# FFN down products of four pairs of blocks by seven half-size products, and squares of the first norm on ScalarE, in a two-layer fp32 decoder trunk

## The chip, the cores and the metric

One core of a Trainium2 chip runs the whole trunk. The metric is the device time of one execution in microseconds; the kernel before has a median of 1934.61 us over 3 runs (1933.79 to 1934.62).

## What is computed

```python
for l in range(DEPTH):                      # DEPTH = 2
    x = x + 0.5 * swiglu(rmsnorm(x, ffn1_norm[l]), ffn1_w_gate[l], ffn1_w_up[l], ffn1_w_down[l])
    x = x + hybrid_mixer(rmsnorm(x, mix_norm[l]), ...)
    x = x + 0.5 * swiglu(rmsnorm(x, ffn2_norm[l]), ffn2_w_gate[l], ffn2_w_up[l], ffn2_w_down[l])

def swiglu(x, w_gate, w_up, w_down):
    return (jax.nn.silu(x @ w_gate) * (x @ w_up)) @ w_down
```

512 tokens, model width 1024, FFN width 2816, everything in float32. There are four FFNs (two a layer). The mixer (sparse attention beside an mLSTM) is not touched.

## The kernel before

Activations are kept transposed: channels on the 128 partitions, the 512 tokens along the free axis, so x is 8 tiles of 128x512 and a matmul streams tokens past a 128x128 piece of weights. To keep float32 accuracy every operand is split in two parts, `hi` (a rounded copy, made by ScalarE) and `lo` (the rest, by a subtraction on VectorE), and every product is three matmuls: hi·hi, hi·lo, lo·hi.

**Weights** come as units of 128x1024 numbers. `fetch` (line 229) loads a unit on SP's queue into a ring of six raw buffers; `unit` (line 263) makes up to two units ahead of the one that it hands out: ScalarE writes `whi` (line 272), VectorE writes `wlo` (line 277). whi and wlo have three buffers each, so the conversion of a unit waits until TensorE is done with the unit three places before it.

**The FFN** is cut into 11 blocks of 256 hidden channels. Blocks 0 and 1 use plain products (`up_plain`). Blocks 2 to 10 compute gate and up in one go by Winograd's form of Strassen's scheme (`quad`, line 476; its list is PRODUCTS): seven products of 24 matmuls of 256 columns, in place of eight. The sums of weight quarters that the scheme needs (s1 to s4) are made by GpSimd on raw units (`form`, line 249: four 128x1024 operations a block); the sums of token parts (t1 to t4) are made once an FFN by `combine`. `assemble` reads the PSUM banks on ScalarE and VectorE, applies Silu and the product of gate and up (`put`, line 498), and splits h into hi and lo (lines 499, 500).

**Groups.** GROUPS pairs the blocks: (0), (1, 2), (3, 4), (5, 6), (7, 8), (9, 10). The down product of a pair is four plain units (`ffn_down`, line 532): each makes two output tiles of 128x512 from four pieces of h, 24 matmuls of 512 columns, and VectorE adds each tile to x straight from PSUM (line 545). `ffn_plan` (line 188) places the four units of a pair between the seven products of the two blocks of the next pair.

**Order.** TensorE runs in the order in which the code is written. On the other engines a scheduling layer sorts by priority (`high_priority` raises it); each engine then works strictly in the order that comes out. `norm` (line 315) squares x, sums the squares on GpSimd (line 334) and splits x times the gain; in the first norm of the program the squares are made by VectorE (line 330), elsewhere by ScalarE (line 332).

In the text a **period** is the stretch from the first product of the first block of one of the pairs (3, 4), (5, 6), (7, 8), (9, 10) to the same place of the next one. Each period holds 14 products and the down work of the pair before. There are four in an FFN and 16 in all.

Of the kernel before, what the change touches and what calls it, by code (L numbers as in the profile page):

```python
# [42 lines left out]
DOWNS = {(1, 1): (), (5, 0): ((3, 0), (5, 1)), (5, 1): ((7, 2), (7, 3))}  # L43
# [16 lines left out]
class Trunk:  # L60
# [5 lines left out]
    def run(self):  # L66
        tc = self.tc
        with tc.tile_pool(name="const", bufs=1) as self.cp, \
# [8 lines left out]
            with tc.manual_schedule(engines={mybir.EngineType.PE}):  # L77
                for l in range(DEPTH):
                    self.norm(self.g1[l], LAG["ffn"] if l else LAG["ffn0"], l == 0)
# [30 lines left out]
    def setup(self):  # L110
        nc, cp, t = self.nc, self.cp, self.t
        self.x = []
# [46 lines left out]
        with self.tc.high_priority(offset=20000):  # L159
            for i in range(NKT):  # L160
                xt = cp.tile([P, S], F32, name=f"x{i}", tag=f"x{i}")
                nc.sync.dma_start(xt, t["x"][i])
                self.x.append(xt)
                if i in START:
                    self.fetch()
# [22 lines left out]
    def ffn_plan(self):  # L188
        plan = [("U", 0, i) for i in range(4)]
        plan += [("U", 1, 0), ("U", 1, 1), ("D", 0, 0), ("D", 0, 1), ("U", 1, 2), ("U", 1, 3)]  # L190
        for gi in range(1, len(GROUPS)):
            for i, b in enumerate(GROUPS[gi]):
                if b == 1:
                    continue
                at = DOWNS.get((gi, i), ((3, 0), (5, 1)) if i == 0 else ((2, 2), (5, 3)))
                for p in range(7):
                    plan += [("D", gi - 1, u) for n, u in at if n == p]
                    plan.append(("Q", b, p))
                plan += [("D", gi - 1, u) for n, u in at if n == 7]
# [10 lines left out]
    def ffn_units(self, l, n):  # L210
        t = self.t
        for kind, b, i in self.plan:
# [3 lines left out]
            elif kind == "D":  # L216
                self.add(t["wda" + n][l, i] if b == 0 else t["wdb" + n][l, b - 1, i], dma=b == 0)
            else:
# [21 lines left out]
    def plain(self, i, n):  # L240
        return self.got(i)[:, :n]

# [72 lines left out]
    def norm(self, g, ffn=0, first=False):  # L315
# [6 lines left out]
        for i in range(NKT):  # L322
# [95 lines left out]
    def ffn(self):  # L418
        h = {}
        quad = None  # L420
        for kind, b, i in self.plan:
            gi = b if kind == "D" else (b + 1) // 2
            if kind != "D" and gi not in h:
                nf = 2 * len(GROUPS[gi])
                tags = ("zah", "zal") if gi % 2 else ("kT", "big")
                h[gi] = None
            if kind == "U":
# [3 lines left out]
                if i == 3:  # L431
                    if b == 0:
                        h[gi] = [self.ap_.tile([P, 2, S], F32R, name="h0", tag="s4b", bufs=2) for _ in range(2)]
                        with self.tc.high_priority(offset=500):
                            self.gate_plain(ps, h[gi])
                    else:
                        h[gi] = [self.ap_.tile([P, nf, S], F32R, name=t, tag=t) for t in tags]
                        next(self.rest)
# [709 lines left out]
```

## Time and profile before

| | |
|---|---|
| median of 3 runs | 1934.61 us |
| the profiled execution | 1933.71 us |
| its span, first to last instruction | 1931.9 us |
| TensorE busy | 98% of the span |
| VectorE, ScalarE, GpSimd busy | 71%, 50%, 28% |
| granted TensorE clock, mean | 0.994 of full speed |

The profiled execution is within 0.05% of the median. The 1.8 us between its own time and its span lie outside the first and last instruction. Matmuls overlap one another, so the duration of one (283 ns for 256 columns) is longer than its distance to the next; what counts is the distance.

### The profile page before, as it was taken

How to read it: one execution, taken by the hardware profiler on the slowest of the kernel's cores; microseconds unless marked ns; L12 is line 12 of the kernel's file. 1: busy time of each engine (PE TensorE's matmuls, PEld its weight loads, DVE VectorE, ACT ScalarE, POOL GpSimd, SP SyncE). 2: the span in 40 equal slices, each digit the busy share in tenths (PEclk: the TensorE clock that was granted, in tenths of full speed). 3: DMA queues.
4: the chain of work that ended last, by engine and by line, in shares of the span. 5: the costliest groups of instructions: out<-in, count | busy, mean ns of one | idle time of the engine just before them, and what ended most of it. 6: DMA issues, size and time to landing. Idle time of an engine off the chain costs nothing.

```text
span 1931.9 us, 29548 instructions
## 1 busy us (share of the span) xinstructions
PE 1898.5 (98%) x11712; PEld 1703.2 (88%) x11712; DVE 1381.1 (71%) x2228; ACT 957.8 (50%) x1495; POOL 543.8 (28%) x335
## 2 busy tenths in 40 slices
PE   7999999999999999999999999999999999999999
PEld 5899999887888899999989999998877888999997
DVE  5976666679955876666788666665898558766665
ACT  3543434477775544343454343435777655434332
POOL 3433323212112242324124423322211122432330
PEclk8999999999999999999999999999999999999999
DMA  6423323375446622323353323334744465332322
GB/s 200 119 83 115 109 88 118 109 159 126 88 91 154 158 99 77 130 78 120 110 141 89 120 79 118 104 110 127 157 107 87 104 142 130 109 118 80 130 68 88
DMA packets 63067, 219.28 MB, mean 114 GB/s; under 512 B 8272, under 2 KB 8784, under 8 KB 62928
## 3 DMA queue, kind: packets, MB, share of 16 engines
q1 hardware_dynamic: 51120, 176.34, 27.1%
q0 software_dynamic: 11232, 40.90, 13.1%
q8 instruction: 92, 1.51, 0.3%
q10 hardware_dynamic: 576, 0.15, 0.1%
q14 instruction: 47, 0.39, 0.1%
HBM read 215.27 MB, written 2.10 MB: 113 GB/s over the span
## 4 chain that ended last, share of the span: by engine, by line
PE 86%; DVE 7%; ACT 4%; issue 1%; POOL 1%; DMA 1%; ACTq 0%; SPq 0%; POOLq 0%; DVEq 0%
PE mm L489 35%; PE aux L294 27%; PE mm L294 22%; DVE wlo L277 1%; PE op L294 1%; DVE qk L956 1%; ACT whi L272 1%; DVE sc L840 1%; DVE m L839 1%; PE aux L889 1%; POOL ws L249 1%; ACT wlo L274 1%; ACT lg L908 0%; DMA raw<-wg_dram 0%; DVE lg L906 0%
## 5 line engine op out<-in xcount | busy, mean ns | idle before, releaser
L272 ACT ACTIVATE whi<-raw 128x1024 fp32r<-128x1024 f32 (+1 forms) x292 | 308.3, 1056 | 471.8 <-PE aux L294 194.1
L277 DVE TENSOR_TENSOR wlo<-raw,whi 128x1024 fp32r<-128x1024 f32 (+1 forms) x214 | 286.2, 1337 | 100.0 <-ACT whi L272 96.0
L249 POOL TENSOR_TENSOR ws<-raw 128x1024 f32<-128x1024 f32 x72 | 194.7, 2704 | 543.4 <-DVE wlo L277 457.6
L489 PE MATMUL mm<-yh,whi 128*128 128x256 f32 x1152 | 326.2, 283 | 0.0
L489 PE MATMUL mm<-yh,wlo 128*128 128x256 f32 x1152 | 326.0, 283 | 0.0
L489 PE MATMUL mm<-yl,whi 128*128 128x256 f32 x1152 | 326.0, 283 | 0.0
L277 DVE TENSOR_TENSOR wlo<-ws,whi 128x1024 fp32r<-128x1024 f32 x144 | 220.7, 1533 | 95.2 <-ACT whi L272 94.9
L272 ACT ACTIVATE whi<-ws 128x1024 fp32r<-128x1024 f32 x144 | 152.8, 1061 | 267.2 <-PE mm L489 131.5
L489 PEld LDWEIGHTS mm<-yh,whi 128*128 128x128 f32 x1152 | 221.0, 192 | 1.6
L489 PEld LDWEIGHTS mm<-yl,whi 128*128 128x128 f32 x1152 | 221.0, 192 | 1.2
L489 PEld LDWEIGHTS mm<-yh,wlo 128*128 128x128 f32 x1152 | 221.0, 192 | 0.0
L545 DVE SCALAR_TENSOR_TENSOR x<-aux,x 128x512 f32<-128x512 f32 x192 | 130.7, 687 | 125.6 <-PE aux L294 125.3
L489 PE MATMUL mm<-qT,whi 128*128 128x256 f32 x1152 | 209.1, 283 | 0.5
L489 PEld LDWEIGHTS mm<-qT,whi 128*128 128x128 f32 x1152 | 181.4, 192 | 3.4 <-issue 1.2
L489 PE MATMUL mm<-qT,wlo 128*128 128x256 f32 x576 | 163.0, 283 | 0.0
L294 PE MATMUL aux<-zah,whi 128*128 128x512 f32 x384 | 149.8, 390 | 0.0
L294 PE MATMUL aux<-zal,whi 128*128 128x512 f32 x384 | 149.8, 390 | 0.0
L294 PE MATMUL aux<-zah,wlo 128*128 128x512 f32 x384 | 149.4, 389 | 0.0
L249 POOL TENSOR_TENSOR ws<-ws,raw 128x1024 f32<-128x1024 f32 x36 | 89.1, 2475 | 116.2 <-issue 115.9
L489 PEld LDWEIGHTS mm<-qT,wlo 128*128 128x128 f32 x576 | 110.4, 192 | 0.0
L294 PE MATMUL mm<-yh,whi 128*128 128x512 f32 x256 | 105.9, 414 | 0.0
L489 PE MATMUL mm<-s4a,whi 128*128 128x256 f32 x576 | 105.5, 283 | 0.0
(289 smaller groups left out, 4264.8 us busy)
## 6 DMA issues: line engine op xcount, KB each, us to landing
raw<-wg_dram SPq DMA_DIRECT2D x88, 512.0 KB, 3.5
raw<-wu_dram SPq DMA_DIRECT2D x88, 512.0 KB, 3.6
raw<-wdb_dram SPq DMA_DIRECT2D x80, 512.0 KB, 3.6
raw<-w_qk_dram SPq DMA_DIRECT2D x16, 512.0 KB, 3.2
wlo<-w_qk_dram POOLq DMA_DIRECT2D x16, 512.0 KB, 5.5
raw<-w_out_dram SPq DMA_DIRECT2D x16, 512.0 KB, 3.2
wlo<-w_out_dram POOLq DMA_DIRECT2D x16, 512.0 KB, 5.8
raw<-wda_dram SPq DMA_DIRECT2D x8, 512.0 KB, 3.4
```

The source lines that it names most:

```text
L249: self.tc.keep_in_program_order(self.nc.gpsimd.tensor_tensor(out=out, in0=x, in1=y, op=op))
L272: nc.scalar.activation(hi[:, :n], raw, AF.Copy)
L274: nc.scalar.activation(lo[:, :n], hi[:, :n].bitcast(F32), AF.Copy, scale=-1.0)
L277: nc.vector.tensor_tensor(out=lo[:, :n], in0=raw, in1=hi[:, :n].bitcast(F32), op=ALU.subtract)
L294: self.nc.tensor.matmul(ps, lhsT, rhs, start=start, stop=stop)
L489: nc.tensor.matmul(ps[:, f, :], a[:, c], r, start=first and f == 0 and k == 0 and n == 0, stop=k == 3 and n == 2, skip_group_check=True)
L545: nc.vector.scalar_tensor_tensor(self.x[d], ps, 0.5, self.x[d], op0=ALU.mult, op1=ALU.add)
L839: nc.vector.max(out=m8, in_=sc)
L840: nc.vector.match_replace(out=sc, in_to_replace=m8, in_values=sc, imm_value=MARK)
L889: nc.tensor.transpose(pt[:, j * P:(j + 1) * P], it["lg"][:, j * P:(j + 1) * P], self.ident)
L956: nc.vector.scalar_tensor_tensor(o, raw[:, k:k + S], w[:, k:k + 1], o, op0=ALU.mult, op1=ALU.add)
```

## The change

The down products of the pairs (1, 2), (3, 4), (5, 6) and (7, 8) go over to the same seven-product scheme. The 512 output channels that two units cover (u = 0 or 1) are one scheme: the unit x holds 256 output channels, its halves a11 (block b) and a12 (block b+1); the unit y holds the other 256, a21 and a22. On the side of h, b11 and b12 are the two token halves of block b, b21 and b22 those of block b+1. GpSimd makes s1 = a21 + a22, s2 = s1 - a11 (one unit, w1) and s3 = a11 - a21, s4 = a12 - s2 (one unit, w2) in operations of 128x512. `put` keeps h unsplit in `he`; `first` and `second` form t1 = b12 - b11, t2 = b22 - t1, t3 = b22 - b12, t4 = t2 - b21; `hsplit` splits seven forms instead of four pieces, into a ring of eight. t1, t3 and t4 are made by GpSimd, t2 by VectorE. `down_quad` runs the seven products in two parts: part 0 is b11, t2, t1, b21 (48 matmuls of 256 columns), part 1 is t3, t4, b22 (36). The results go to x by six VectorE operations that read PSUM, one ScalarE copy and three GpSimd additions a scheme. The unit w1 is fetched with one unit less ahead, as x and w1 are held together. CHUNKS and LASTCH place the parts: in a period of a middle pair, part 0 before product 2, part 1 before product 4 and the second part 0 after product 6 of the first block, the second part 1 before product 4 of the second.

In the first norm of the program ScalarE squares x instead of VectorE. The x tiles are allocated in pairs. Blocks 0, 9 and 10 keep plain down products.

```diff
+CHUNKS = {0: ((2, 0, 0), (4, 0, 1), (7, 1, 0)), 1: ((4, 1, 1),)}
+LASTCH = {0: ((2, 0, 0), (4, 0, 1)), 1: ((2, 1, 0), (7, 1, 1))}
+FORMS = ("t1", "b11", "b21", "t2", "t3", "t4", "b22")
...
+    def dform(self, nm, d):
...
+        x, y = self.got(d["x"]), self.got(d["y"])
+        a11, a12, a21, a22 = x[:, :S], x[:, S:], y[:, :S], y[:, S:]
+        if nm == "a22":
+            return a22
+
+        def comb(out, p, q, op):
+            self.tc.keep_in_program_order(self.nc.gpsimd.tensor_tensor(out=out, in0=p, in1=q, op=op))
+
+        w = self.ap_.tile([P, UN], F32, name="wd", tag={"w1": "stk", "w2": "sc"}[nm])
+        if nm == "w1":
+            d["w1"] = w
+            comb(w[:, S:], a21, a22, add)
+            comb(w[:, :S], w[:, S:], a11, sub)
+        else:
+            comb(w[:, :S], a11, a21, sub)
+            comb(w[:, S:], a12, d["w1"][:, :S], sub)
+        return w
...
-            if first:
-                nc.vector.tensor_tensor(out=sq, in0=self.x[i], in1=self.x[i], op=ALU.mult)
-            else:
-                nc.scalar.activation(sq, self.x[i], AF.Square)
+            nc.scalar.activation(sq, self.x[i], AF.Square)
...
+    def hsplit(self, gi, nm, src):
...
+        nc.scalar.activation(t[:, 0], src, AF.Copy)
+        nc.vector.tensor_tensor(out=t[:, 1], in0=src, in1=t[:, 0].bitcast(F32), op=ALU.subtract)
+        self.hform[gi, nm] = t
...
+    def first(self, gi, e):
+        t1 = self.piece("wi")
+        self.nc.gpsimd.tensor_tensor(out=t1, in0=e[:, 1], in1=e[:, 0], op=ALU.subtract)
+        self.hsplit(gi, "t1", t1)
+        self.t1 = t1
+
+    def second(self, gi, e1, e2, sh):
+        nc = self.nc
+        if sh == 0:
+            self.hsplit(gi, "b11", e1[:, 0])
+            self.hsplit(gi, "b21", e2[:, 0])
+            return
+        t2 = self.piece("wt")
+        nc.vector.tensor_tensor(out=t2, in0=e2[:, 1], in1=self.t1, op=ALU.subtract)
+        self.hsplit(gi, "t2", t2)
+        nc.gpsimd.tensor_tensor(out=e1[:, 1], in0=e2[:, 1], in1=e1[:, 1], op=ALU.subtract)
+        self.hsplit(gi, "t3", e1[:, 1])
+        nc.gpsimd.tensor_tensor(out=e2[:, 0], in0=t2, in1=e2[:, 0], op=ALU.subtract)
+        self.hsplit(gi, "t4", e2[:, 0])
+        self.hsplit(gi, "b22", e2[:, 1])
+
+    def down_quad(self, gi, u, part):
...
+        def mul(w, o, nm, ps, first):
+            hi, lo = w
+            t = self.hform[gi, nm]
+            for j in range(2):
+                for k in range(2):
+                    c = slice(o + k * FB + j * P, o + k * FB + (j + 1) * P)
+                    for n, (a, r) in enumerate(((hi, 0), (hi, 1), (lo, 0))):
+                        nc.tensor.matmul(ps[:, j, :], a[:, c], t[:, r, k, :],
+                                         start=first and j == 0 and k == 0 and n == 0,
+                                         stop=k == 1 and n == 2, skip_group_check=True)
+                self.tick()
...
+        if part == 0:
+            d = self.dq = {}
+            w = self.unit()
+            d[0] = bank("aux")
+            mul(w, 0, "b11", d[0], True)
+            with self.tc.high_priority(offset=300):
+                d["q"] = tile("cv")
+                nc.scalar.activation(d["q"], d[0], AF.Copy)
+            v = self.unit(1)
+            d[1] = bank("aux")
+            mul(v, 0, "t2", d[1], True)
+            with self.tc.high_priority(offset=300):
+                u2 = tile("hn")
+                nc.vector.tensor_tensor(out=u2, in0=d[1], in1=d["q"], op=ALU.add)
+                add(0, 1, u2, nc.gpsimd)
+            d[2] = bank("aux")
+            mul(v, S, "t1", d[2], True)
+            mul(w, S, "b21", d[0], False)
+            with self.tc.high_priority(offset=300):
+                add(0, 0, d[0], nc.vector)
+        else:
+            d = self.dq
+            w = self.unit()
+            mul(w, 0, "t3", d[1], False)
+            with self.tc.high_priority(offset=300):
+                u3 = tile("cv")
+                nc.vector.tensor_tensor(out=u3, in0=d[1], in1=d["q"], op=ALU.add)
+                add(1, 1, d[2], nc.vector)
+                add(1, 0, u3, nc.gpsimd)
+                add(1, 1, u3, nc.gpsimd)
+            v = self.unit(1)
+            d[3] = bank("op")
+            mul(v, 0, "t4", d[3], True)
+            with self.tc.high_priority(offset=300):
+                add(1, 0, d[3], nc.vector, ALU.subtract)
+            mul(w, S, "b22", d[2], False)
+            with self.tc.high_priority(offset=300):
+                add(0, 1, d[2], nc.vector)
...
         def put(g, u, sh):
+            if gi < len(GROUPS) - 1:
+                e = h[b]
+                nc.vector.scalar_tensor_tensor(e[:, sh], u, 0.5, g, op0=ALU.mult, op1=ALU.mult)
+                if b == GROUPS[gi][1]:
+                    self.second(gi, h[b - 1], e, sh)
+                elif sh:
+                    self.first(gi, e)
+                return
```

The built programs give these orders. Before, GpSimd's queue in a middle period holds the four operations of each block and nothing else (`ws` is a sum of weight quarters):

```order
L249 TENSOR_TENSOR ws_1038<-raw_540,raw_579 128x1024
L249 TENSOR_TENSOR ws_908<-raw_778,ws_908 128x1024
L249 TENSOR_TENSOR ws_1212<-raw_1046,raw_1109 128x1024
L249 TENSOR_TENSOR ws_1214<-ws_1212,raw_1044 128x1024
L249 TENSOR_TENSOR ws_1344<-raw_1044,raw_1046 128x1024
```

The same queue in the changed kernel, at the start of the period of blocks 5 and 6 (`he` is unsplit h: the two L527 and L529 rows are t3 and t4 of blocks 3 and 4; `wd_1726` is the unit w1 and `wd_1825` the unit w2 of the first scheme):

```order
L286 TENSOR_TENSOR ws_1648<-ws_1646,raw_1456 128x1024
L527 TENSOR_TENSOR he_954<-he_1378,he_954 128x512
L529 TENSOR_TENSOR he_1378<-wt_1682,he_1378 128x512
L268 TENSOR_TENSOR wd_1726<-raw_1573 128x512
L268 TENSOR_TENSOR wd_1726<-wd_1726,raw_1523 128x512
L541 TENSOR_TENSOR x0_131<-x0_131,dq_1792 128x2x256
L268 TENSOR_TENSOR wd_1825<-raw_1523,raw_1573 128x512
L268 TENSOR_TENSOR wd_1825<-raw_1523,wd_1726 128x512
```

The two rows of w1 stand behind t3 and t4, and the two rows of w2 behind an addition to x.

Further on in the same period, where its first block ends (`wi_2053` is t1 of block 5, `dq_2089` the sum u2 of the second scheme; `ws_2119` and `ws_2121` are s1 and s2 of block 6):

```order
L268 TENSOR_TENSOR wd_2018<-wd_2018,raw_1893 128x512
L514 TENSOR_TENSOR wi_2053<-he_1694 128x512
L541 TENSOR_TENSOR x4_139<-x4_139,dq_2089 128x2x256
L286 TENSOR_TENSOR ws_2119<-raw_1947,raw_1949 128x1024
L286 TENSOR_TENSOR ws_2121<-ws_2119,raw_1945 128x1024
```

The sums s1 and s2 of the next block now stand behind t1 and an addition to x. In the period of the last pair this second place differs: there s1 and s2 stand ahead of the addition, and no t1 is made.

VectorE at the start of that period, in the changed kernel (`tmp_1678` reads the last product of block 4, `lg_1608` times it is h, `wt_1682` is t2, the `hf` rows are lo parts of forms):

```order
L690 TENSOR_TENSOR tmp_1678<-mm_1490,lg_1447 128x512
L314 TENSOR_TENSOR wlo_1696<-raw_1523,whi_1695 128x1024
L653 SCALAR_TENSOR_TENSOR he_1378<-lg_1608,tmp_1678 128x512
L525 TENSOR_TENSOR wt_1682<-he_1378,wi_1313 128x512
L506 TENSOR_TENSOR hf_688<-he_1378,hf_688 128x512
L506 TENSOR_TENSOR hf_686<-wt_1682,hf_686 128x512
L506 TENSOR_TENSOR hf_687<-he_954,hf_687 128x512
L506 TENSOR_TENSOR hf_687<-he_1378,hf_687 128x512
```

The first three rows stand where their counterparts stood; t2 and four subtractions on forms follow them.

## Rows read from the trace of the kernel before

**Rows 1.** The page, part 1: busy time, share of the span, instructions.

```profile
PE 1898.5 (98%) x11712; PEld 1703.2 (88%) x11712; DVE 1381.1 (71%) x2228; ACT 957.8 (50%) x1495; POOL 543.8 (28%) x335
```

**Rows 2.** Stretches by engine, one period: length, busy us and instructions of PE, PEld, DVE, ACT, POOL, clock, DMA.

```profile
157.40:219.60 62.20, 62.20 (x435) 58.37 (x434) 41.41 (x44) 24.59 (x29) 19.65 (x8) 1.00 0.30 102
```

**Rows 3.** The chain that ended last, by time: start, us, what; the same period.

```profile
171.80 5.47 PE aux L294 x24
177.27 5.75 PE mm L489 x48
```

**Rows 4.** Timeline at a block's first matmul: start, us, engine, line, operation [idle before].

```profile
163.00 0.28 PE L489 MATMUL mm<-yh,whi 128*128 128x256 f32 x1
...
163.13 1.06 ACT L272 ACTIVATE whi<-raw 128x1024 fp32r<-128x1024 f32 x1 [0.72 <-PE mm L489]
...
163.39 0.68 DVE L528 TENSOR_TENSOR tmp<-mm,lg 128x512 f32<-128x512 f32 x1
...
164.11 0.63 ACT L529 ACTIVATE tmp<-tmp 128x512 f32<-128x512 f32 x1
...
164.22 1.22 DVE L277 TENSOR_TENSOR wlo<-raw,whi 128x1024 fp32r<-128x1024 f32 x1
...
165.37 0.68 DVE L498 TENSOR_TENSOR lg<-lg,tmp 128x512 f32<-128x512 f32 x1
```

**Rows 5.** Timeline of GpSimd: a 1024-wide and a 512-wide operation with nothing beside them.

```profile
142.64 2.40 POOL L249 TENSOR_TENSOR ws<-raw,ws 128x1024 f32<-128x1024 f32 x1
...
622.17 1.30 POOL L334 TENSOR_TENSOR tmp<-tmp 128x512 f32<-128x512 f32 x1 [2.02 <-ACT tmp L332]
```

**Rows 6.** Timeline of VectorE and GpSimd, 67.9 to 75.4 us, in `combine`.

```profile
67.93 2.40 POOL L249 TENSOR_TENSOR ws<-raw 128x1024 f32<-128x1024 f32 x1 [2.19 <-PE aux L294]
...
68.71 2.17 DVE L385 TENSOR_TENSOR yc<-yc,ys 128x512 f32<-128x512 f32 x1
...
70.41 2.73 POOL L249 TENSOR_TENSOR ws<-ws,raw 128x1024 f32<-128x1024 f32 x1
...
70.81 3.41 DVE L277 TENSOR_TENSOR wlo<-raw,whi 128x1024 fp32r<-128x1024 f32 x1
...
74.14 0.68 DVE L385 TENSOR_TENSOR yc<-yc,ys 128x512 f32<-128x512 f32 x1
...
74.74 0.68 DVE L395 TENSOR_TENSOR yl<-yc,yh 128x512 fp32r<-128x512 f32 x1
```

**Rows 7.** Groups by line: VectorE's additions to x that read PSUM (busy, mean ns).

```profile
L545 DVE SCALAR_TENSOR_TENSOR x<-aux,x 128x512 f32<-128x512 f32 x192 | 130.7, 687 | 125.6 <-PE aux L294 125.3
```

**Rows 8.** Timeline of TensorE around two idle spells in the mixer.

```profile
451.42 0.33 PE L889 MATMUL aux<-zid,lg 128*128 128x128 f32 x1 [1.26 <-ACT lg L908]
...
516.86 1.47 PE L294 MATMUL mm<-va,qk 128*128 128x129 f32 x6 [2.04 <-ACT qk L1004]
```

**Rows 9.** Stretches by engine after each of these two spells, columns as in rows 2.

```profile
449.00:453.00 4.00, 2.74 (x15) 1.97 (x13) 4.00 (x15) 3.97 (x9) 1.39 (x2) 1.00 0.00 0
...
517.20:520.60 3.40, 3.40 (x12) 2.91 (x11) 3.40 (x15) 1.03 (x3) 0.09 (x1) 0.50 0.67 131
520.60:524.00 3.40, 3.40 (x25) 3.09 (x24) 2.15 (x8) 1.20 (x3) 0.00 (x0) 1.00 0.00 0
```

**Rows 10.** Timelines of the first norm: VectorE, GpSimd, TensorE, columns as in rows 4.

```profile
14.16 1.89 DVE L330 TENSOR_TENSOR tmp<-x 128x512 f32<-128x512 f32 x3
...
26.79 1.75 DVE L336 SCALAR_TENSOR_TENSOR qT<-x,g,qT 128x512 fp32r<-128x512 f32 x1
...
23.05 7.98 POOL L334 TENSOR_TENSOR tmp<-tmp 128x512 f32<-128x512 f32 x5
...
28.59 0.79 PE L294 MATMUL mm<-qT,whi 128*128 128x512 f32 x1 [9.15 <-DVE qT L336]
...
31.08 1.22 PE L294 MATMUL aux<-ones,tmp 128*128 128x1 f32 x5
```

**Rows 11.** Groups by line: ScalarE's squares in the later norms (busy, mean ns).

```profile
L332 ACT ACTIVATE tmp<-x 128x512 f32<-128x512 f32 x40 | 25.2, 631 | 56.6 <-DVE x L545 38.3 <-DVE x L1075 18.3
```

More of the change, by code (lines that the diff above doesn't have):

```diff
@@ L111, in setup @@
         nc, cp, t = self.nc, self.cp, self.t
-        self.x = []
+        self.x, self.x2 = [], []
         self.stream = []
@@ L194, in ffn_plan @@
                     continue
[L195 to L199, printed above, removed]
+                at = () if gi == 1 else (LASTCH if gi == len(GROUPS) - 1 else CHUNKS)[i]
+                for p in range(8):
+                    plan += [("S", gi - 1, (u, c)) for n, u, c in at if n == p]
+                    if p < 7:
+                        plan.append(("Q", b, p))
         return plan + [("D", len(GROUPS) - 1, u) for u in range(4)]
@@ L313, in rsqrt, with norm @@
         return r
-    def norm(self, g, ffn=0, first=False):
+    def norm(self, g, ffn=0):
         nc = self.nc
@@ L420, in ffn @@
         quad = None
+        self.hform = {}
+        self.ring = None
+        last = len(GROUPS) - 1
         for kind, b, i in self.plan:
[L422 to L426, printed above, removed]
+            gi = b if kind in "DS" else (b + 1) // 2
             if kind == "U":
@@ L432, in ffn @@
                     if b == 0:
[L433 removed]
+                        h[b] = [self.ap_.tile([P, 2, S], F32R, name="h0", tag="s4b", bufs=2) for _ in range(2)]
                         with self.tc.high_priority(offset=500):
[L435 removed]
+                            self.gate_plain(ps, h[b])
                     else:
[L437 removed]
@@ L438, in ffn @@
                         next(self.rest)
+                        self.ring = [self.ap_.tile([P, 2, 2, 2, H], F32R, name="hf", tag=t)
+                                     for t in ("kT", "big", "zah", "zal")]
+                        h[b] = self.stage()
                         with self.tc.high_priority(offset=500):
-                            self.gate_plain(ps, h[gi])
+                            self.gate_plain(ps, None, h[b])
+                            self.first(gi, h[b])
             elif kind == "D":
-                self.ffn_down(h[gi], 2 * len(GROUPS[gi]), i)
+                self.ffn_down([h[k] for k in GROUPS[gi]], 2 * len(GROUPS[gi]), i)
+            elif kind == "S":
+                self.down_quad(gi, *i)
@@ L443, in ffn, with final @@
             else:
                 if i == 0:
-                    if h[gi] is None:
-                        h[gi] = [self.ap_.tile([P, nf, S], F32R, name=t, tag=t) for t in tags]
                     quad = {}
-                self.quad(quad, i, h[gi], 2 * (b - GROUPS[gi][0]))
+                    if gi < last:
+                        h[b] = self.stage()
+                    else:
+                        h[b] = self.final(gi, b)
+                self.quad(quad, i, gi, b, h)
+    def final(self, gi, b):
+        if b == GROUPS[gi][0]:
+            return [self.ap_.tile([P, 2, S], F32R, name="hl", tag="so", bufs=2) for _ in range(2)]
+        n = [(7 * (gi - 1) + FORMS.index(nm)) % 8 for nm in ("b11", "t1")]
+        return [self.ring[i // 2][:, i % 2].rearrange("p a f s -> p (a f s)").rearrange("p (f s) -> p f s", s=S)
+                for i in n]
```

58 lines of the change are left out of this document (47 added, 11 removed).

## The prediction

> **What bounds the kernel now.** I read the page first [rows 1]: TensorE is busy 98% of the span, VectorE 71%, ScalarE 50%, GpSimd 28%. A share over the whole program says little of one stage, so next come the stretches by engine, for one period [rows 2]: in 62.20 us TensorE is busy 62.20, VectorE 41.41, ScalarE 24.59, GpSimd 19.65. Conversions, evictions and sums all fit beside the matmuls there. The chain by time [rows 3] gives the distance between matmuls: 5.47 us for 24 of 512 columns is 227.9 ns, 5.75 us for 48 of 256 columns is 119.8 ns. The 16 periods make 16 x 62.2 = 995 us, half of the run; outside them the change does little. So the questions are what TensorE saves in a period, and whether the other engines, in their new order, still deliver in time.
>
> **TensorE.** A scheme replaces two units of 24 matmuls: 48 x 227.9 ns = 10.94 us. It issues 7 x 12 = 84 of 256 columns: 84 x 119.8 ns = 10.06 us. The 32 schemes (2 a period) save 32 x 0.88 = 28.0 us, and a period's matmuls take 62.2 - 1.8 = 60.4 us. The scheme removes an eighth of the columns, but the shorter matmul pays its fixed part twice as often [rows 3]. The Trainium skill (TensorE: Matmul & The Clock Gate, Back-to-back issue gap) gives columns / 2.4 + 2.5 ns, that is 215.8 and 109.2 ns; by it the saving would be 38 us, and the trace does not agree: its fixed part is about 14 ns, so the measured distances stand.
>
> **Work beside it, a period.** VectorE: 18 conversions of 1024 become 20 and two of 512; 26 operations of 512 become 34 (12 for h where 8 were, 12 for evictions where 8 were, 10 in `assemble` as before). From start to next start 1024 takes 1.15 us [rows 4] and 512 takes 0.60 [rows 6]: 36.3 us become 20 x 1.15 + 36 x 0.60 = 44.6. GpSimd: its 8 operations of 1024 get 17 of 512 as company (8 weight sums, 3 forms, 6 additions to x): 19.2 us become 8 x 2.40 + 17 x 1.30 = 41.3 [rows 5]. ScalarE: two more copies of 1024 and seven of 512, 2 x 1.06 + 7 x 0.63 = 6.5 us [rows 4], some 31 of 62 us, free of charge except in the two chains below. The same weights are loaded. SP's queue holds x and y from part 0 to part 1, so two of its six buffers fetch less far ahead; what hides that is that the sums s1 and s2 start late anyway (second place). By shares everything fits; by order it does not.
>
> **First place, the start of all 16 periods.** Let T be the first matmul of a period. A start as it is now [rows 4]: the last product's assembly runs from T+0.39 (L528), Silu from T+1.11, a conversion from T+1.22, and the product of gate and up (L498) ends at T+3.05. The changed order of VectorE keeps these and puts t2 next: T+3.7. GpSimd's queue then has t3, t4 (which needs t2) and only behind them the two sums of w1. Four operations at 1.25 to 1.30 us, with four lo subtractions of forms at 0.55 taking turns with them (the port, below), end at 3.7 + 5.0 + 2.2 = T+10.9. ScalarE's copy, 1.06 us [rows 4], makes whi at T+12.0. TensorE wants it after two products and b11: 2 x 2.88 + 1.44 = T+7.2. It waits 4.8 us. wlo takes 1.2 us more and the third matmul needs it: 1.0 more. Without port turns it is T+9.5 for whi: 2.3 + 1.0 us. I take the larger, as both engines have all their inputs by then.
>
> **Second place, the end of the first block, in the three middle periods of each FFN (12).** Let A be the start of the second scheme's part 0. h is ready at A+3.05 [rows 4]. GpSimd: t1, the addition of u2 to x4 (u2 waits for the product t2, A+2.9, and one VectorE operation), then s1 and s2 of the next block: 3.05 + 2 x 1.30 + 2 x 2.26 with two subtractions of 0.55 between, A+11.4; whi at A+12.5. TensorE wants it at A + 4 x 1.44 + 2.88 = A+8.64: it waits 3.9 us, and 1.0 for wlo (without port turns 2.9 + 1.0). Before, nothing stood ahead of s1 and s2. In the last pair's period the addition stands behind them, so I charge nothing.
>
> **The clock.** After an idle spell of 2.04 us the granted clock was 0.50 for 3.4 us; after one of 1.26 us it stayed at 1.00 [rows 8, 9]. Both waits are longer than 2.04, so each adds a stretch at half speed, partly under the wait for wlo: 1.1 us each (bounds 0 and 1.7). A first place costs 4.8 + 1.0 + 1.1 = 6.9 us, a second 3.9 + 1.0 + 1.1 = 6.0.
>
> **The chains alone:** 16 x 6.9 + 12 x 6.0 - 28.0 = +154.4 us. Periods of 60.4 + 12.9 = 73.3 (three of four) and 67.3: 71.8 on average.
>
> **The port, the other price of a period.** In `combine` [rows 6] VectorE's `yc` (two inputs in SBUF) starts at 68.71 and ends at 70.88, 0.55 after GpSimd's operation ends (70.33). GpSimd's next ends at 73.14, 2.26 after `yc`; the conversion behind it ends 1.08 later, 3.41 us long where it takes 1.22 alone [rows 4]. The two engines exclude each other when VectorE reads two operands from SBUF. Operations that read PSUM do not wait (687 ns on average over 192) [rows 7]. So in a period GpSimd holds the port for 8 x 2.26 + 17 x 1.16 = 37.8 us (1.16 is 1.30 less what 2.40 has over 2.26), and VectorE for 20 x 1.08 + 14 x 0.55 = 29.3: 67.1 us, above the 60.4 of TensorE. Before: 18.1 + 18 x 1.08 + 8 x 0.55 = 41.9. VectorE's other 22 operations, 13.2 us, can run under GpSimd's, but wait in order behind blocked ones. If half of them do (GpSimd holds the port half of the period), a period is 37.8 + 44.6 - 6.6 = 75.8 us; all 69.2, near the port's 67.1; none 82.4.
>
> The chain walk treats VectorE as free elsewhere, which the port forbids; the port ledger at one half is a guess. I take the middle of 71.8 and 75.8: **73.8 us a period**.
>
> **First norm.** TensorE idles 9.15 us before 28.59 for the last lo part of y [rows 10], which waits its turn behind squares and GpSimd's sums. With squares on ScalarE (8 x 0.63 us) [rows 11] that part is ready near 18 us. The next need is the sum of squares at 31.08: seven additions of 1.3 to 1.6 us from some 15 us on end at 25 to 26. I take 5 us of gain (bounds 0 and 9).
>
> **Sum:** 16 x (73.8 - 62.2) - 5 = +180.6 us against the profiled execution's own 1933.7: 2114 us. The median of the runs stands 0.9 us above that execution, which I leave aside.
>
> **Rivals.**
> 1. *TensorE still sets the pace; faster.* The chain at T ends before T+7.2, and likewise at A. Price: 1933.7 - 28.0 - 5 = 1901 us. It decides where four GpSimd operations fit in (7.2 - 3.05 - 1.15) / 4 = 0.75 us each. For: GpSimd has been idle 68% of a period. Against: 1.30 us [rows 5], and the order. Chance 0.07; 0.02 more for a result within 0.2% of the time before (about what a measurement of this kernel can tell from no change), where waits would just cancel the gain.
> 2. *The port alone decides and both queues are always full.* Periods of 67.1 us: 16 x 4.9 - 5 = +73, 2007 us. The Trainium skill (SBUF — State Buffer, Who interferes with whom) states this as its one rule: a VectorE operation with two SBUF inputs and a GpSimd operation that reads SBUF lock each other out for the whole instruction. The trace agrees with the lock (0.55 and 1.08 us after the other's end) [rows 6]. For: it needs no guess on order. Against: fixed orders leave both idle at times. Chance 0.13.
> 3. *Nothing overlaps.* VectorE's operations on PSUM all stand behind blocked ones: 82.4 us a period, 2252 us. For: VectorE is in order and TensorE's results come in bursts. Against: evictions reach the head of the queue while GpSimd works in the stretch before too. Chance 0.08.
>
> That the change does not do what it says is excluded by the order: 84 matmuls a scheme, squares on ScalarE.
>
> **How the numbers follow.** The forecast has 0.70. Its own range goes from the chains without port turns and clock (16 x 3.3 + 12 x 3.9 - 28 - 5 = +67, 2000 us) to a third of the PSUM operations hidden (about 78 us a period, 2181) and some unforeseen waits, 2195. This takes in rival 2; rival 3, rival 1 and no change, 0.17, stay out. Faster 0.07, same 0.02, slower 0.91.
>
> **What would show it.** In the stretches of a period TensorE should be busy near 60 of some 74 us, VectorE's and GpSimd's conversions and sums should be longer than alone (1.22, 2.40, 1.30), TensorE's waits should name the conversions of w1 and of s2, at two places of a middle period and one of the last, and the clock should fall to 0.50 behind them. Part 0's second product should start some 12 us after the period. The first sum of squares should come near 26 us. I am wrong if TensorE is busy over 98% of a period, if its waits name DMAs or PSUM banks, or if GpSimd's 512-wide operations take well under 1 us.

## The result and the profile after

The changed kernel takes 2256.07 us (median of 4 runs, 2253.6 to 2257.19) against 1934.61 us before: ratio 1.166, 95% interval 1.165 to 1.168. That is 321 us slower, where 180 were forecast; 2256 lies outside the range of 2000 to 2195. The span of the profiled execution is 2251.9 us, 320 more than before, and its mean granted clock 0.939.

The page, part 1, of the changed kernel answers to [rows 1]:

```profile
PE 1995.9 (89%) x12864; PEld 1841.1 (82%) x12864; DVE 1679.1 (75%) x2412; ACT 1052.1 (47%) x1647; POOL 980.4 (44%) x607
```

The stretches by engine of two middle periods, columns as in [rows 2]:

```profile
182.00:265.70 83.70, 68.83 (x507) 67.58 (x506) 60.50 (x57) 30.24 (x37) 46.80 (x25) 0.89 0.22 76
265.70:349.50 83.80, 68.96 (x507) 67.61 (x506) 58.58 (x57) 30.13 (x37) 47.74 (x25) 0.90 0.22 76
```

No engine is full: TensorE lacks 15 us of a period, VectorE 23 to 25, GpSimd 36 to 37. From the spans, with the 5.2 us that the first norm gives (first experiment), a period grew on average by (320.0 + 5.2) / 16 = 20.3 us, to 82.5. Now TensorE's waits in the whole execution (engine, line, what it waited for: us in total, times, longest):

```profile
PE mm L643 <- DVE lg L683: 89.7, 28, 3.7
PE aux L553 <- ACT whi L309: 63.9, 16, 5.3
PE mm L643 <- ACT whi L309: 42.3, 12, 3.5
PE mm L643 <- DVE wlo L314: 20.3, 20, 1.8
PE aux L553 <- DVE wlo L314: 10.0, 16, 1.1
```

The second line is the first place, 16 times; the third is the second place, 12 times. The first place goes as it was walked: in the period whose first matmul starts at 182.03, the four operations of GpSimd end 10.2 us after it (forecast 10.9) and whi is made at 11.3 (12.0), as the timelines of TensorE, GpSimd and ScalarE show:

```profile
182.03 0.41 PE L643 MATMUL mm<-yh,whi 128*128 128x256 f32 x1
...
185.40 1.80 POOL L527 TENSOR_TENSOR he<-he 128x512 f32<-128x512 f32 x1 [6.56 <-DVE he L653]
...
190.67 1.59 POOL L268 TENSOR_TENSOR wd<-wd,raw 128x512 f32<-128x512 f32 x1
...
192.29 1.06 ACT L309 ACTIVATE whi<-wd 128x1024 fp32r<-128x1024 f32 x1 [2.71 <-POOL wd L268]
```

The line with the most time was in no step of the forecast: 28 times, product s4 waits for `c22` (line 683), which reads the bank that s4 adds to. Call it the **third place**: seven an FFN, one in each block of the four periods but the last one's second. Its history, on GpSimd, VectorE and ScalarE, and TensorE's end of the wait (the timeline, columns as in [rows 4]):

```profile
166.25 0.69 DVE L587 TENSOR_TENSOR dq<-aux,dq 128x512 f32<-128x512 f32 x1
167.02 2.56 POOL L541 TENSOR_TENSOR x<-x,dq 128x512 f32<-128x512 f32 x2 [8.33 <-DVE dq L587]
169.52 3.40 POOL L286 TENSOR_TENSOR ws<-raw,ws 128x1024 f32<-128x1024 f32 x1
...
172.95 1.06 ACT L309 ACTIVATE whi<-ws 128x1024 fp32r<-128x1024 f32 x1 [5.05 <-POOL ws L286]
...
174.04 2.30 DVE L314 TENSOR_TENSOR wlo<-ws,whi 128x1024 fp32r<-128x1024 f32 x1 [2.79 <-ACT whi L309]
176.27 0.68 DVE L681 TENSOR_TENSOR lg<-mm,pT 128x512 f32<-128x512 f32 x1
...
176.98 0.69 DVE L683 TENSOR_TENSOR lg<-mm,lg 128x512 f32<-128x512 f32 x1
...
177.81 0.48 PE L643 MATMUL mm<-qT,whi 128*128 128x256 f32 x2 [3.69 <-DVE lg L683]
```

GpSimd stands idle for 8.33 us, because the two additions of u3 to x are next in its queue and u3 comes at 166.9. The sum for s4, whose raw inputs had been there, stands behind them. From then on each step is late: sum, whi, wlo, and behind wlo in VectorE's order u3 and c22 of the quad. GpSimd's own waits in the whole execution show the same:

```profile
POOL x L541 <- DVE dq L587: 199.4, 32, 10.4
POOL x L541 <- DVE dq L574: 125.8, 20, 10.3
POOL he L527 <- DVE he L653: 105.0, 16, 6.6
POOL wi L514 <- DVE he L653: 93.7, 12, 7.9
```

At the additions alone GpSimd idles 325 us, at t1 and t3 another 199. Behind the wait at 177.81 the clock falls (stretches by engine, columns as in [rows 2]; they answer to [rows 9]):

```profile
173.90:177.80 3.90, 0.22 (x2) 0.03 (x2) 3.72 (x4) 1.06 (x2) 2.68 (x2) 1.00 0.72 269
177.80:181.20 3.40, 3.39 (x21) 3.40 (x22) 3.37 (x4) 1.06 (x1) 1.05 (x1) 0.69 0.00 0
181.20:184.60 3.40, 3.40 (x25) 3.40 (x25) 3.40 (x5) 2.32 (x3) 0.00 (x0) 0.80 0.02 5
184.60:188.00 3.40, 3.40 (x30) 3.40 (x30) 3.37 (x5) 2.27 (x4) 2.60 (x2) 1.00 0.00 0
```

From the clock's records in the trace TensorE spends 276 us at the lower level (0.50, or 1.2 GHz), in 61 pieces; before, 24 us in 4. The matmuls in these pieces take 91.6 us more than at the distances of [rows 3] (before 3.0). The idle spells between matmuls add up to 270 us (before 31). So the bookkeeping is -28 (matmuls saved) +240 (idle) +89 (clock) = +301 of the +320. The norm's 5 us are no term of their own, as they lie inside the idle time and the clock. The other 19 are in spells that this count leaves out, those shorter than one more matmul distance above all.

### The profile page after: what moved, and what is told of

The parts are those of the page before. It is cut to its first block, busy times and chain, and to the rows that moved or that the text cites. A ratio compares the mean times of both kernels' runs of the same rounds, so it can differ in the third digit from the quotient of the medians.

```text
span 2251.9 us, 32675 instructions
## 1 busy us (share of the span) xinstructions
PE 1995.9 (89%) x12864; PEld 1841.1 (82%) x12864; DVE 1679.1 (75%) x2412; ACT 1052.1 (47%) x1647; POOL 980.4 (44%) x607
## 5 line engine op out<-in xcount | busy, mean ns | idle before, releaser
L309 ACT ACTIVATE whi<-raw 128x1024 fp32r<-128x1024 f32 (+2 forms) x292 | 293.1, 1004 | 291.6 <-PE mm L643 99.5
L643 PE MATMUL mm<-yh,whi 128*128 128x256 f32 x1152 | 338.7, 294 | 42.3 <-ACT whi L309 42.3
L553 PE MATMUL aux<-hf,whi 128*128 128x256 f32 x1536 | 312.4, 303 | 63.9 <-ACT whi L309 63.9
L643 PE MATMUL mm<-qT,whi 128*128 128x256 f32 x1152 | 251.8, 320 | 90.1 <-DVE lg L683 89.7
L314 DVE TENSOR_TENSOR wlo<-raw,whi 128x1024 fp32r<-128x1024 f32 (+2 forms) x214 | 310.3, 1451 | 20.9 <-ACT whi L309 20.8
L553 PEld LDWEIGHTS aux<-hf,whi 128*128 128x128 f32 x1536 | 265.0, 212 | 67.1 <-ACT whi L309 67.1
L541 POOL TENSOR_TENSOR x<-x,dq 128x512 f32<-128x512 f32 x96 | 128.1, 1350 | 325.2 <-DVE dq L587 199.4
L553 PE MATMUL aux<-hf,wlo 128*128 128x256 f32 x768 | 234.7, 306 | 10.0 <-DVE wlo L314 10.0
L643 PEld LDWEIGHTS mm<-yh,wlo 128*128 128x128 f32 x1152 | 232.3, 202 | 11.0 <-DVE wlo L314 10.9
L553 PEld LDWEIGHTS aux<-hf,wlo 128*128 128x128 f32 x768 | 162.0, 211 | 14.8 <-DVE wlo L314 14.4
L309 ACT ACTIVATE whi<-wd 128x1024 fp32r<-128x1024 f32 x64 | 67.8, 1059 | 150.3 <-POOL wd L268 103.7
L506 DVE TENSOR_TENSOR hf<-he,hf 128x512 fp32r<-128x512 f32 x80 | 123.5, 1559 | 0.0
```

The source lines that it names most:

```text
L309: nc.scalar.activation(hi[:, :n], raw, AF.Copy)
L314: nc.vector.tensor_tensor(out=lo[:, :n], in0=raw, in1=hi[:, :n].bitcast(F32), op=ALU.subtract)
L506: nc.vector.tensor_tensor(out=t[:, 1], in0=src, in1=t[:, 0].bitcast(F32), op=ALU.subtract)
L541: eng.tensor_tensor(out=x(r, sh), in0=x(r, sh), in1=v, op=op)
L553: nc.tensor.matmul(ps[:, j, :], a[:, c], t[:, r, k, :], start=first and j == 0 and k == 0 and n == 0, stop=k == 1 and n == 2, skip_group_c ...
L643: nc.tensor.matmul(ps[:, f, :], a[:, c], r, start=first and f == 0 and k == 0 and n == 0, stop=k == 3 and n == 2, skip_group_check=True)
```

## Experiments

Each run was compared with the kernel before on the same chip (1933.75 to 1934.48 us). Waits of TensorE in us, from the view shown above: behind c22 (third place), for whi of w1 (first place), for whi of the sums s1 to s4 (second place), for wlo (both lines); last, its time at the lower clock. A place can also wait for parts of h (hf), which the table leaves out.

| run | us | ratio, 95% interval | c22 | whi w1 | whi s | wlo | low clock |
|---|---|---|---|---|---|---|---|
| changed kernel | 2256.1 | 1.165 to 1.168 | 89.7 | 63.9 | 42.3 | 30.3 | 276 |
| e1 norm only | 1928.7 | 0.997 to 0.999 | | | | | |
| e2 additions on VectorE | 2215.1 | 1.144 to 1.148 | 69.6 | 62.8 | 27.2 | 39.8 | 252 |
| e3 t1, t3, t4 on VectorE | 2179.8 | 1.125 to 1.129 | 70.4 | 8.0 | 43.3 | 47.0 | 191 |
| e4 both | 2115.6 | 1.092 to 1.097 | 107.0 | 0 | 0 | 23.9 | 176 |
| e5 s1 copied | 2247.4 | 1.160 to 1.163 | 0 | 92.7 | 52.7 | 81.7 | 276 |
| e6 e4 and s1 copied | 2086.8 | 1.077 to 1.083 | 0 | 0 | 0 | 117.3 | 20 |
| e7 e3 and s1 copied | 2179.4 | 1.125 to 1.128 | 0 | 8.1 | 53.5 | 103.5 | 168 |
| e12 two writes for an addition | 2283.1 | 1.179 to 1.182 | 118.3 | 65.8 | 36.7 | 29.3 | 327 |
| e17 one write for an addition | 2183.2 | 1.127 to 1.131 | 49.1 | 76.3 | 27.9 | 33.3 | 228 |
| e13 no additions | 2120.1 | 1.095 to 1.098 | 0 | 73.5 | 22.4 | 39.8 | 193 |
| e14 e6 without additions | 2045.9 | 1.057 to 1.060 | 0 | 0 | 0 | 62.6 | 56 |
| e15 additions later | 2186.0 | 1.128 to 1.132 | 3.0 | 96.8 | 32.0 | 41.1 | 249 |
| e16 e15 and e3 | 2100.3 | 1.084 to 1.087 | 3.0 | 0 | 0 | 70.5 | 117 |

**The norm alone (e1).** The kernel before with the one line of the norm changed:

```diff
-                    self.norm(self.g1[l], LAG["ffn"] if l else LAG["ffn0"], l == 0)
+                    self.norm(self.g1[l], LAG["ffn"] if l else LAG["ffn0"])
```

> The kernel before with only the squares of the first norm moved from VectorE to ScalarE. In the profile of the changed kernel the sum of squares reaches TensorE at 25.12 us instead of 31.08 and the first seven-product matmul starts at 73.96 instead of 78.79. Theory: the gain is the part's own and independent of the down products: about 4.8 us less than before, 1930 us. Rival: it only shifts a wait that the down products' change would have shifted anyway (the table products left the queue of GpSimd there): less than 2 us.

Measured 1928.74 us (1928.19 to 1929.28), 5.2 less. The sum of squares now reaches TensorE at 26.84 (31.08 in [rows 10]):

```profile
26.84 1.87 PE L294 MATMUL aux<-ones,tmp 128*128 128x1 f32 x8 [7.98 <-POOL tmp L334]
```

The term of 5 us stands, and this version is faster than both kernels.

**Work off GpSimd's queue (e2, e3, e4).**

```diff
-                add(0, 1, u2, nc.gpsimd)
+                add(0, 1, u2, nc.vector)
...
-        self.nc.gpsimd.tensor_tensor(out=t1, in0=e[:, 1], in1=e[:, 0], op=ALU.subtract)
+        self.nc.vector.tensor_tensor(out=t1, in0=e[:, 1], in1=e[:, 0], op=ALU.subtract)
```

e2 has the first for all three additions of a scheme, e3 the second for t1, t3 and t4, e4 both.

> The changed kernel with the six additions to x a period moved from GpSimd to VectorE. Queue theory (TensorE waits because late work stands ahead of weight sums in GpSimd's order): the third place (28 waits before a product with h in qT, 89.7 us of idle, each behind s4, which stands behind two additions) goes nearly, the second place (12 waits, 42.3 us) loses about 1.3 of 3.5 us each, the first (16 waits, 63.9 us) stays; with the half clock behind the waits that go, 120 to 150 us less than the changed kernel: 2105 to 2135. Port theory (what counts is how long the two engines hold the port in a period, 67.1 us by the ledger): 6 x (1.16 - 0.55) = 3.7 us a period, 59 us less: about 2197, with waits spread over all places.

> The changed kernel with t1, t3 and t4 moved from GpSimd to VectorE. Queue theory: the first place goes (63.9 us of idle for whi, 10.0 for wlo, about a quarter of the 91 us that the half clock costs), the second loses t1's 1.3 us each, the third stays at 28 waits: 95 to 125 us less than the changed kernel: 2130 to 2160. Port theory: 3 x 0.61 = 1.8 us a period, 29 us less: about 2227.

> Both moves: GpSimd keeps the weight sums alone. Queue theory: all three places go, the clock stays at full speed, a period falls to between 60.4 us (matmuls alone) and 64, the whole to 1900 to 1960 us. Port theory: 9 x 0.61 = 5.5 us a period less than the changed kernel, about 2168 us; the port ledger alone (27.4 + 34.3 = 61.7 us a period) would allow no less than 1920.

e2 gave 41 us, e3 76 and e4 140; the queue theory in its first form had wanted more from each. It holds for what it was made of: in e3 the wait for whi of w1 falls from 63.9 to 8.0 us (the one for its wlo rises from 10.0 to 29.1), in e4 the waits for whi at the first and the second place are gone. But the third stays, and grows in e4. In e2 and e4 the additions stand on VectorE, ahead of u3 and c22 of the quad, and the scheduler has also put a 1024-wide conversion between these two, which it had not in the changed kernel.

**The bank freed early (e5, e6, e7).** ScalarE copies the bank behind product s1, so that s4 needn't wait for c22.

```diff
+        elif nm == "s1":
+            q["c22"] = tile("tmp")
+            nc.scalar.activation(q["c22"], ps, AF.Copy)
...
-            q["c22"] = tile("lg")
-            nc.vector.tensor_tensor(out=q["c22"], in0=q[2], in1=q["u3"], op=ALU.add)
+            c22 = tile("lg")
+            nc.vector.tensor_tensor(out=c22, in0=q["c22"], in1=q["u3"], op=ALU.add)
+            q["c22"] = c22
```

> The changed kernel with one thing different: ScalarE copies the bank of product s1 into SBUF right behind that product, and c22 is summed from the copy, so product s4 no longer waits for VectorE to read that bank. Nothing moves between GpSimd and VectorE. Theory (three separate waits of TensorE in a period, each set by its own chain): the 28 waits of the product that follow c22 (89.7 us) go, and with them their share of the stretches at half clock, some 46 us; the 32 waits for w1's conversion (63.9 and 10.0) and the 12 for s2's (42.3) stay: about 2120 us (2090 to 2160). Rival (TensorE is late by a fixed amount, because the port between GpSimd and VectorE paces the period): another wait takes the place of the one removed, above all for whi and wlo of the same product, and the time stays above 2200 us. Second rival: c22 now reads two operands in SBUF, so it takes turns with GpSimd and is late, and the waits for h grow instead; then it is within 1% of the changed kernel.

> The s1 copy on ScalarE together with the additions to x and the forms t1, t3, t4 on VectorE. Theory (queues: with the three waits gone nothing holds TensorE): 2115.6 less the 107 us of waits behind c22 and the half-clock share of them, some 55: 1950 us (1920 to 1990). Rival (port: 61.7 us a period of locked operations, and VectorE with 63 us of work of its own in a period): VectorE itself becomes the bound; waits for wlo and for h take the place: 2040 to 2110 us.

> The s1 copy on ScalarE and t1, t3, t4 on VectorE; the additions to x stay on GpSimd. Theory (three separate waits): of the 2179.8 us of the kernel with the forms moved alone, the 70.4 us of waits behind c22 and their half-clock share, some 32, go: about 2075 us (2050 to 2110); the 43.3 us for s2's conversion stay. Rival (port or a fixed lateness): the time stays within 2% of 2179.8.

The theory of three separate waits falls, as the rivals of e5 and e7 had it: e5 gains 9 us, e7 nothing. The c22 waits are gone, but TensorE now waits for wlo, or later for w1. c22 was only the last link; the link before it, the conversion of s4's sum, is nearly as late. In e6 the waits of all three places are gone and TensorE's waits in the periods name conversions, nearly all VectorE's (117.3 us for wlo, 20.6 for lo parts of h, against 8.1 for ScalarE's hi parts); 2086.8 us is in the rival's range. Two periods of e6 (stretches by engine, columns as in [rows 2]):

```profile
118.50:190.00 71.50, 62.48 (x506) 60.85 (x505) 70.10 (x65) 31.21 (x41) 36.92 (x17) 1.00 0.25 89
190.00:264.10 74.10, 64.98 (x507) 63.76 (x506) 70.30 (x65) 31.47 (x41) 37.10 (x17) 0.95 0.25 86
```

VectorE is busy 70 of 71.5 and 74.1 us (its turns with GpSimd lengthen its operations and so count as busy): there it comes nearest to setting the pace.

**The additions' place, length and reads (e12, e17, e13, e14).** In e13 the three additions of a scheme are left out. In e12 and e17 writes of a constant to the tile of u2 or u3 keep their place and their wait:

```diff
-                add(0, 1, u2, nc.gpsimd)
+                for _ in range(2):
+                    self.tc.keep_in_program_order(nc.gpsimd.memset(u2, 0.0))
```

(e12; e17 has one write for each addition.)

> The changed kernel, in which the six GpSimd additions of u2 and u3 to x in a period are left out; in the place of each, two writes of a constant to the tile of u2 or u3 stand in GpSimd's queue, which wait for the same VectorE result (0.53 us each, as measured: 1.06 for an addition's 1.35). So the queue keeps its order and its waits, and the two engines' turns in SBUF for these six go. If the turns pace the period (port theory): a good part of what leaving the additions out gives: 2150 to 2190 us. If only places and waits in GpSimd's queue count: within 1.5% of the changed kernel (2225 to 2256).

> The changed kernel without the six GpSimd additions of u2 and u3 to x in a period (left out, nothing in their place). Theory (GpSimd and VectorE fill the period together): 6 x 1.35 us a period x 16 = 130 us and some of the half-clock stretches: 2100 to 2140 us, far below the 2215 us that moving them to VectorE gave. Rival (what counts is one wait at the bank of c22 behind VectorE's queue): it stays near 2215.

> The version with t1, t3, t4 on VectorE and the s1 copy on ScalarE, with the six additions left out that stood on VectorE in it (2086.8 us with them; their mean there 1.19 us, worked out from 0.90 over all seven additions to x in a scheme, four of them 0.68). Theory (VectorE's own time, 95% of the period, paces that version): 6 x 1.19 x 16 = 114 us less: 1960 to 1990 us. Rival (GpSimd's sums pace it): within 1% of 2087.

> The changed kernel, in which the six GpSimd additions of u2 and u3 to x in a period are left out; in the place of each, one write of a constant to the tile of u2 or u3 (0.53 us instead of 1.35, no read). GpSimd still waits there for the same VectorE result, and VectorE's order is that of the changed kernel. If the wait at the head of GpSimd's queue is what costs: the c22 waits stay (over 50 of the 89.7 us) and the time is 2180 to 2240 us. If the additions' length and their turns at the port cost: near the version with the additions left out, 2120 to 2150 us.

Without the additions (e13) 136 us come back and the c22 waits are gone, although c22 and its bank are as they were. e12 doesn't decide: the scheduler put a conversion between u3 and c22 there, too, as the timeline of VectorE in e12 shows at the same place:

```profile
174.94 0.68 DVE L682 TENSOR_TENSOR lg<-mm,pT 128x512 f32<-128x512 f32 x1
175.54 3.03 DVE L314 TENSOR_TENSOR wlo<-raw,whi 128x1024 fp32r<-128x1024 f32 x1
178.49 0.68 DVE L684 TENSOR_TENSOR lg<-mm,lg 128x512 f32<-128x512 f32 x1
```

In e17 VectorE's order is that of the changed kernel, but for three additions to x that change places once an FFN (the same in e13 and e15). It splits the 136 us: 73 go with the additions' length and reads (0.53 us without a read for 1.35 with two), 63 stay with what e17 keeps, the wait at the head of the queue and the 0.53 us of each write. That the waits behind c22 stay was expected at over 50 us; they are 49.1. In e14 the additions are taken from VectorE: 41 us less where 114 were expected. VectorE's busy time falls by 58 us (1821.2 to 1763.0) and not by the 110.6 that the additions took in e6, as other operations became longer: its conversions of w1 and w2 take 1.88 us on average, in e6 1.47 (64 of them). But the order of VectorE's operations changed with it (c22 among them), so e14 is no test of one thing, and that VectorE's time alone paces e6 is not shown.

**The additions later (e15, e16).** All work stays on its engine; the additions wait in a list until the next sums have been issued.

```diff
-                add(1, 0, u3, nc.gpsimd)
-                add(1, 1, u3, nc.gpsimd)
+                self.late += [(x(1, 0), u3), (x(1, 1), u3)]
...
         nm, tn, bank, first = PRODUCTS[i]
         hi, lo = self.unit()
+        self.flush()
```

`flush` issues the additions in the list on GpSimd; u2's goes the same way.

> The changed kernel with all of its work on the same engines; only the six GpSimd additions of u2 and u3 to x in a period stand later in GpSimd's queue: u3's two behind the sum for s4, u2's behind the next pair of sums. Theory (GpSimd idles 325 us at the head of its queue for u2 and u3, while sums that TensorE needs stand behind): the waits behind c22 (89.7 us) go, GpSimd's idle time before the additions falls under 50 us, and the time comes near the version without the additions, 2120 us, plus part of their own 128 us: 2120 to 2190. Rival (the amount of work on GpSimd and VectorE counts, not its place): 2230 to 2260.

> The same, with t1, t3 and t4 on VectorE. Theory: what moving the forms gave in the changed kernel (76 us) comes on top, as far as VectorE has room (its conversions there take longer): 2050 to 2110 us, TensorE waiting mainly for VectorE's wlo and hf. Rival (both engines full): within 1% of e15.

Order alone gives 70 us (2185.95), and 156 with the forms on VectorE. The c22 waits fall from 89.7 us to 3.0. GpSimd's idle time before the additions falls from 325 us to 147, not under 50 (groups by line; busy, mean ns, idle before and its releasers):

```profile
L536 POOL TENSOR_TENSOR x<-x,dq 128x512 f32<-128x512 f32 x96 | 161.0, 1691 | 147.2 <-DVE x L547 114.9 <-DVE dq L580 32.2
```

Each addition takes 1.69 us instead of 1.35, and the wait for w1 grows by 33 us: what is moved takes its turn elsewhere.

**The port by itself (e8, e9).** The kernel before with 14 operations more a period on GpSimd, which nobody waits for (252 in all; `scrap` is a spare tile):

```diff
...
+        self.tc.keep_in_program_order(nc.gpsimd.tensor_tensor(out=self.scrap, in0=self.scrap, in1=self.scrap,
+                                                              op=ALU.mult))
```

In e9 two writes (`memset`) stand in place of the multiplication.

> The kernel before, with 14 more GpSimd operations in a period that nobody waits for: one multiplication of a spare 512-wide tile by itself behind each product, in SBUF (about 1.3 us each by the kernel before). Nothing else changes, the schemes for down included: they are not in it. Port theory (such operations and VectorE's two-input operations exclude each other, so they delay conversions and evictions): VectorE's conversions of 1024 rise from a mean of 1.37 us to over 1.6, TensorE waits in the periods, and the kernel is slower by 1 to 4% (1955 to 2010 us). Rival (only the order behind GpSimd's queue costs): as fast as its twin that writes constants in place of the multiplications, within 0.3%.  If both are at 1934, the port and the queue of this size cost nothing as long as nobody waits for the operations.

> The twin of the run with 14 multiplications: in place of each of them two writes of a constant to the same 512-wide tile by GpSimd, which read nothing (about 0.5 us each, estimated from 204 ns for 128 columns and 98 ns for 3 in the trace of the kernel before). They take a similar place in GpSimd's queue. Port theory: within 0.3% of the kernel before (1934 us), VectorE's conversions as before. Rival (the queue): as slow as its twin.

e8 takes 1962.22 us, ratio 1.0154 (1.0138 to 1.0169); e9 1935.16 us, 1.0009 (0.9999 to 1.0018). VectorE's wide conversions, of units as loaded and of sums (groups by line; busy us, mean ns), of the kernel before:

```profile
L277 DVE TENSOR_TENSOR wlo<-raw,whi 128x1024 fp32r<-128x1024 f32 x206 | 277.3, 1346 | 100.0 <-ACT whi L272 96.0
L277 DVE TENSOR_TENSOR wlo<-ws,whi 128x1024 fp32r<-128x1024 f32 x144 | 220.7, 1533 | 95.2 <-ACT whi L272 94.9
```

of e8:

```profile
L277 DVE TENSOR_TENSOR wlo<-raw,whi 128x1024 fp32r<-128x1024 f32 x206 | 361.6, 1760 | 47.5 <-ACT whi L272 45.5
L277 DVE TENSOR_TENSOR wlo<-ws,whi 128x1024 fp32r<-128x1024 f32 x144 | 239.1, 1661 | 106.0 <-ACT whi L272 105.6
```

and of e9:

```profile
L277 DVE TENSOR_TENSOR wlo<-raw,whi 128x1024 fp32r<-128x1024 f32 x206 | 319.3, 1550 | 99.0 <-ACT whi L272 96.3
L277 DVE TENSOR_TENSOR wlo<-ws,whi 128x1024 fp32r<-128x1024 f32 x144 | 176.4, 1225 | 96.8 <-ACT whi L272 92.8 <-PE aux L294 3.6
```

VectorE's order in both is that of the kernel before. The 350 conversions together take 498 us before, 601 in e8 and 496 in e9; one group alone misleads, as in e9 the first grew by what the second lost. Reads cost 27 us more than writes in a similar queue (372 us of multiplications on GpSimd against 267 of writes). The Trainium skill (SBUF — State Buffer, Who interferes with whom) says that a VectorE operation with two SBUF inputs contends with a GpSimd operation that reads SBUF and not with one that only writes it; these two runs agree. So the exclusion is real, but in a kernel whose queues have slack 14 reads a period cost 28 us in all, under a tenth of the 321.

**Low parts by DMA (e10, e11).** A remedy that failed: the low part of the eight weights a period that are used as loaded comes from a DMA.

```diff
-                    self.jobs.append((self.dform, ("x", d), False))
+                    self.jobs.append((self.dform, ("x", d), True))
...
-                self.jobs.append((self.form, (form, q), False))
+                self.jobs.append((self.form, (form, q), form in ('a11', 'a12', 'a22')))
...
```

> The changed kernel, but the low part of 8 of the 20 wide conversions of a period (the weight blocks that are used as they are loaded: a11, a12, a22 of gate and up, x of down) no longer comes from VectorE's subtraction: ScalarE writes the negated high part and a DMA issued by GpSimd adds the weight from DRAM, as the kernel does already for the mixer's weights. GpSimd's sums and additions stay where they are, with 10 issues of some 0.87 us more in its queue. Theory (VectorE and GpSimd together fill the period because their SBUF operations take turns): VectorE has 8 x 1.5 us less, the waits for wlo and behind c22 shrink: 2080 to 2160 us. Rival (GpSimd's queue alone sets it): the issues lengthen that queue: 2250 to 2320 us.

> The same low parts by DMA, on top of the version with the additions to x and t1, t3, t4 on VectorE and the s1 copy on ScalarE, in which VectorE is busy 95% of the stretches of the periods and TensorE waits only for VectorE (wlo, hf). Theory (VectorE's time, with its turns at the port, is what paces that version): 8 conversions of 1.68 us a period leave, 13 us, more than the 9 that TensorE lacks to 60.4: TensorE sets the pace again, 1905 to 1940 us, which may beat the kernel before. Rival (latency: the DMA's 5.5 us and the queue of GpSimd come late instead): TensorE waits for wlo by DMA, 1980 to 2090 us.

2426.68 us (ratio 1.253 to 1.257) and 2320.04 (1.199 to 1.202), beyond the rivals' ranges, too. TensorE's waits in e10:

```profile
PE mm L644 <- DMA wlo<-wu_dram: 130.4, 36, 6.1
PE mm L644 <- DMA wlo<-wg_dram: 110.5, 48, 3.5
PE aux L554 <- DMA wlo<-wdb_dram: 88.0, 22, 5.1
```

The issue waits in GpSimd's queue for ScalarE's negated copy (585.8 us in 127 waits, the mixer's among them), and the landing takes 5.4 us more; made two units ahead (some 5.8 us of TensorE), that is too late.

## Why the prediction was wrong

- **Direction: right, and the mechanism in the main.** The matmuls saved are worth little, and GpSimd's in-order queue makes the sums late.
- **First place: right.** Forecast 4.8 and 1.0 us, 16 times; measured 63.9 / 16 = 4.0 and 10.0 / 16 = 0.6. e3 takes t1, t3 and t4 out of the queue and its wait for whi falls to 8.0 us in all.
- **Second place: right.** Forecast 3.9 and 1.0, 12 times; measured 42.3 / 12 = 3.5 and 1.0 (20.3 / 20).
- **The step that failed: that these two places are all** ("the chains alone"). The part on the second place walks the addition of u2 ahead of s1 and s2. The additions of u3, two at a time, stand in the same way ahead of s4's sum, 28 times, and were counted only as 1.30 us of work each. Their price is 89.7 us of waiting at TensorE; with the additions out of the way of s4's sum and VectorE's order all but unchanged this wait falls to 0 (e13) and 3.0 us (e15). It is a wait for a PSUM bank, which the prediction had named as a sign of being wrong.
- **The clock: mis-sized.** Forecast 28 x 1.1 = 31 us; measured 89. One piece costs 91.6 / 61 = 1.5 us, inside the bounds of 0 and 1.7; it is the number of pieces that doubled. In the trace 16 of the 61 begin in or behind a wait at the first place and 12 at the second, the 28 of the forecast, and 27 at the third.
- **The port ledger: it does not set the period.** 75.8 us at one half; measured 82.5. The exclusion is shown (e8, e9). But when the additions are moved in the queue with all work left in, 70 us come back (e15), which no ledger of port time allows.
- **Rival 3 gave 2252 us, and the time is 2256.** The agreement is chance: "nothing overlaps" would leave no room for e15, and in the changed kernel VectorE and GpSimd are both idle for 9% of the FFN's stretch (from the trace, 102.2 to 427.4 us).
- **First norm: right.** 5 forecast, 5.2 measured.

With the measured terms the forecast's sum reads -28 - 5 + 74 + 63 + 90 + 89 = +283 (wlo's 20.3 put with the second place). What is left to 320, some 37 us, no run assigns. Some 15 of it may be the way of counting (an estimate): the view counts a wait from the end of a matmul of 0.28 us [rows 4], while matmuls stand 0.12 apart [rows 3], and the three places have 92 waits. How much of the 73 us in e17 is the additions' length and how much their reads stays open. That the scheme could pay with another split of the work is not shown: even without the additions and with the forms on VectorE (e14) the kernel is 5.8% slower than before, with TensorE's waits still mostly for VectorE.

## What to carry over

An operation that waits at the head of an in-order queue costs its wait beside its length (of the 136 us that the additions cost here, 63 stay when each is a short write in the same place): for each operation that a change adds, ask when its input comes and what ready work stands behind it, and do so at every place of the period, not at the first two found. When the last link of a late chain is removed, look how late the link before it is; here that took 90 us of waits away and gave 9 us. A scheduler may move other work when an experiment changes one operation, so compare the order on every engine before a run is read as one change.

## What the hardware showed beyond what was expected

In these runs long waits were paid twice, as waits and at the lower clock, and short ones mostly once. In e6 TensorE idles 193 us in all, no wait in the periods over 2.8 us and 1.2 on average for the most frequent (73.0 / 60), and it spends 20 us at the lower clock. In the changed kernel it idles 270 us in waits of 3.2 to 4.0 us on average at its three places, and spends 276 us there. And a GpSimd operation with two SBUF inputs has no fixed price: the additions to x took 1.35 us in the changed kernel and 1.69 in e15, the sums 2.40 alone [rows 5] and 3.40 beside a conversion.
